# Modulation of all layers as VectorE sums, in halves, run through the mLSTM heads

## The chip, the cores and the metric

One core of a Trainium2 chip runs the whole network in one launch. The metric is the device time of that launch in microseconds. Three runs of the kernel before gave 2507.35, 2513.32 and 2513.51 us; the median is 2513.32. A further execution was profiled, and all rows below are from it.

## The reference, cut to what matters

Two blocks with two layers each process 512 tokens (256 context, 256 latent) of 1024 features, in float32. Block one has an mLSTM layer and a latent attention layer (MLA), each followed by a convolutional FFN; block two has two layers of token mixers, each followed by an MLP. Every layer is modulated by a condition vector: six vectors of 1024 features come from a matrix of 1024 x 6144.

```python
def _modulation(cond, w, b):
    m = jax.nn.silu(cond) @ w + b
    return jnp.split(m[:, None, :], 6, axis=-1)

def _modulate(x, shift, scale):
    return x * (1 + scale) + shift

# per layer: 0 shift, 1 scale, 2 gate of the mixer; 3 shift, 4 scale, 5 gate of the FFN
x = _layer_norm(ALPHA * x + ml[2] * yl, ...)
f = _conv_ffn(_modulate(x, ml[3], ml[4]), ...)
x = _layer_norm(ALPHA * x + ml[5] * f, ...)
```

Latent and context tokens have different conditions, so each vector is computed for two conditions where the context is still needed, else for one. The four matrices hold 96 MB, more than a quarter of what the kernel loads.

## The kernel before, in words

Activations lie transposed, features on the 128 partitions and tokens along the free dimension. Every float32 product is three matmuls of split operands (high and low part): `mm3`, lines 284 to 286. A weight comes in tiles of 512 KB: `weight` (line 266) loads the tile into one of five `raw` buffers by a DMA on SyncE's queue, ScalarE rounds it to the high part (line 278), VectorE subtracts to get the low part (line 279). Three buffers of split weights are shared by all, except for weights that are kept through two halves of the tokens (`keep`), which take room in the pool `ap` of 31 buffers of 4 KB per partition.

The layers are called 0 to 3 here. Their modulation is background work, written as Python generators. `weight` calls `tick(size)` between its load and its split: each call adds credit for the size of the weight (1 for 512 KB) times a rate, and for each whole credit the first generator in the list `bg` is run to its next `yield`. So one step of the modulation is put into the program order between a weight's load and its split. `finish(gen)` runs a generator to its end. A scheduler then orders the instructions of each engine by that program order and by its own estimate of when each is ready; every engine runs its instructions in order.

There are two forms of the background work. A part is one of the six vectors of a layer; its matrix slice comes in 8 chunks of 512 KB, each of 128 input features by 1024 output features.

- `ada_v` (line 430; layers 0, 1 and 3): for each condition an accumulator of 128 x 1024. Per chunk and condition one instruction, accumulator + chunk x condition value of the partition: on ScalarE for the first chunk (line 449), VectorE `scalar_tensor_tensor` for the other seven (line 451). With the last chunk, in the same step, comes the part's end: matmuls with ones of 128 x 32 (line 460), one per condition and 512 features, each on a column tile of its own, sum over the partitions into one PSUM bank (pool `pa`, one buffer); ScalarE copies it (line 464), four transposes (line 467) turn it, and VectorE adds the bias (line 472).
- `ada` (line 396; layer 2): per chunk four column-tiled matmuls of 128 x 32 by 128 x 256 straight from the chunk (line 410), accumulated in PSUM over the eight chunks; at the end a copy (line 416) and two transposes (line 419).

Layer 0's parts 0 and 1 are needed first and are made apart, in `first_mod`. Its parts 2 to 5 run beside the projections `w_up` (rate 0.6) and `w_og` (1.1). In front of the heads `pause` (line 492) runs the open part to its end and stops the background work, which goes on after the heads. Layer 1 runs in the first FFN (rate 0.8), layer 2 behind it in the MLA and the second FFN (1.2), layer 3 in the first MLP (0.8).

The mLSTM (`_mlstm`) projects, computes the gates by scans over time, and then per head: `qk_of` (8 weight tiles), `weights_of` (decay weights, VectorE and ScalarE), later `values_of` (8 tiles) and `head_out`. The gate row of a head is spread over the partitions by a matmul with a row-select table `selr` (line 718), an `ap` buffer copied from a 512 KB input (lines 688 to 691). `weights_of` leaves two `ap` buffers per head, one of them half full.

Of the kernel before, what the change touches and what calls it, by code (L numbers as in the profile page):

```python
# [8 lines left out]
F32 = mybir.dt.float32  # L9
F32R = mybir.dt.float32r  # L10
I32 = mybir.dt.int32
AF = mybir.ActivationFunctionType
ALU = mybir.AluOpType
AX = mybir.AxisListType

P = 128
D = 1024
T = 512
TC = 256
KD = D // P  # L20
# [10 lines left out]
_PV = {}  # L31
# [31 lines left out]
def _lay(I):  # L63
    I = {k: np.asarray(v) for k, v in I.items()}
    o = {}
# [67 lines left out]
    o["sel"] = _sel()  # L133
# [3 lines left out]
def _consts():  # L137

    s = np.arange(P)[:, None]
    j = np.arange(P)[None, :]  # L140
    m0 = np.where(s <= j, 0.0, -1e30)
    m1 = np.where(s >= j, 0.0, -1e30)
    perms = []
    for w in (16, 8):
        pm = np.zeros((P, P))
        for m in range(P):
            if m % (2 * w) < w:
                pm[m + w, m] = -1.0
            else:
                pm[m - w, m] = 1.0  # L150
        perms.append(pm)
    return np.concatenate([np.eye(P), m0, m1] + perms, 1).astype(np.float32)
# [17 lines left out]
def _sel():  # L170
    k = np.arange(P)[:, None, None]
    r = np.arange(8)[None, :, None]
    row = (r % 4) + 32 * (r // 4)
    return np.broadcast_to((k % 64) == row, (P, 8, P)).astype(np.float32)
# [5 lines left out]
class _K:  # L180
    def __init__(self, ctx, tc, A, out):
        self.tc, self.nc, self.A, self.out = tc, tc.nc, A, out
        nc = tc.nc
# [14 lines left out]
        self.credit = 0.0  # L198
        self.hold = self.open = False
# [3 lines left out]
        cst = cp.tile([P, 5 * P], F32, name="cst", tag="cst")  # L203
# [12 lines left out]
        self.mask = (cst[:, P:2 * P], cst[:, 2 * P:3 * P])  # L216

# [178 lines left out]
    def ada(self, l, parts=range(6), mod=None):  # L396


        nc = self.nc
        if mod is None:  # L400
            mod = self.cp.tile([P, 6, KD, 2], F32, name=f"mod{l}", tag=f"mod{l}")
        yield mod
        bo = _PV["ada_b"][0] + 48 * l
        for part in parts:
            ps = self.pa.tile([P, 512], F32, name=self.uid("pa"), tag="pa")
            for kt in range(KD):
                raw = self.rawp.tile([P, 4, 256], F32, name=self.uid("raw"), tag="raw")
                nc.sync.dma_start(raw, self.A["ada"][6 * l + part - 2, kt])
                for j in range(4):
                    nc.tensor.matmul(ps[32 * j:32 * j + 32, 0:256], self.cs[:, l // 2, kt, :],  # L410
                                     raw[:, j, :], start=(kt == 0), stop=(kt == KD - 1),
                                     tile_position=(0, 32 * j))
                if kt < KD - 1:
                    yield
            rows = self.t2()
            nc.scalar.copy(rows[:, 0:256], ps[:, 0:256])
            pt = self.ax_ps()
            for h in range(2):
                nc.tensor.transpose(pt[:, h * P:(h + 1) * P], rows[:, h * P:(h + 1) * P], self.ident)
            m = mod[:, part].rearrange("p (j h) w -> p h j w", h=2)  # L420
            b = self.pv[:, bo + part * KD:bo + (part + 1) * KD].rearrange("p (j h) -> p h j", h=2)
            t = pt[:, 0:256].rearrange("p (h j w) -> p h j w", h=2, j=4)
            for h in range(2):
                nc.vector.tensor_tensor(m[:, h], t[:, h, :, 0:2],
                                        b[:, h].unsqueeze(2).to_broadcast([P, 4, 2]), op=ALU.add)
            if part in (1, 4):
                nc.vector.tensor_scalar(mod[:, part], mod[:, part], 1.0, None, op0=ALU.add)
            yield

    def ada_v(self, l, parts=range(6)):  # L430
# [7 lines left out]
        for part in parts:  # L438
            conds = (1,) if l % 2 and part > 1 else (0, 1)
            nw = len(conds)  # L440

            acc = [self.a4(F32, (P, D)) for _ in conds]
            for kt in range(KD):
                raw = self.rawp.tile([P, D], F32, name=self.uid("raw"), tag="raw")
                nc.sync.dma_start(raw, self.A["ada"][6 * l + part - 2, kt].rearrange("p a b -> p (a b)"))
                for s, w in zip(acc, conds):
                    c = self.cs[:, l // 2, kt, w:w + 1]
                    if kt == 0:
                        nc.scalar.activation(s, raw, AF.Copy, scale=c)
                    else:  # L450
                        nc.vector.scalar_tensor_tensor(s, raw, c, s, op0=ALU.mult, op1=ALU.add)  # L451
                self.open = True
                if kt < KD - 1:
                    yield
            self.open = False

            ng = 32 * 2 * nw
            ps = self.pa.tile([P, 512], F32, name=self.uid("pa"), tag="pa")
            for i in range(2 * nw):
                nc.tensor.matmul(ps[32 * i:32 * i + 32], self.ones[:, 0:32],  # L460
                                 acc[i // 2][:, 512 * (i % 2):512 * (i % 2) + 512],
                                 start=True, stop=True, tile_position=(0, 32 * i))
            rows = self.t2()
            nc.scalar.copy(rows[0:ng], ps[0:ng])
            pt = self.ax_ps()
# [9 lines left out]
            yield  # L475

    def later(self, gen, rate):

        self.bg.append([gen, rate])

    def tick(self, size):
        if not self.bg or self.hold:
            return
        self.credit += self.bg[0][1] * size
        while self.bg and self.credit >= 1.0:
            self.credit -= 1.0
            try:
                next(self.bg[0][0])
            except StopIteration:
                self.bg.pop(0)  # L490

    def pause(self):

        while self.open:
            next(self.bg[0][0])
        self.hold = True

    def finish(self, gen):

        while any(g is gen for g, _ in self.bg):  # L500
            for _ in self.bg.pop(0)[0]:
                pass
# [87 lines left out]
def _mlstm(K, mod, rest):  # L590
# [38 lines left out]
    K.later(rest, 0.6)  # L629
# [8 lines left out]
    K.bg[0][1] = 1.1  # L638
# [49 lines left out]
    selr = K.a4(F32R, (P, 8, P))  # L688
    sel = K.a4(F32, (P, 8, P))
    nc.sync.dma_start(sel, A["sel"])  # L690
    nc.vector.tensor_copy(selr, sel)
# [19 lines left out]

    def weights_of(hd, qp):
# [3 lines left out]
        for d in range(2):  # L716
            ps = K.mm_ps()
            nc.tensor.matmul(ps, selr[:, 4 * d + hd, :], R2, start=True, stop=True)
# [58 lines left out]
        pt = [K.a4(), K.a4(F32, (P, 2, TC))]  # L777
# [75 lines left out]
    K.pause()  # L853
# [41 lines left out]
    K.hold = False  # L895
# [870 lines left out]
def _build(tc, A, out):  # L1766
    with ExitStack() as ctx:
# [7 lines left out]
        gen = K.ada_v(0, (2, 4, 3, 5))  # L1775
        mod = next(gen)
        z, yl = _mlstm(K, mod, gen)
# [4 lines left out]
        gen1 = K.ada_v(1)  # L1782
        mod1 = next(gen1)
        K.later(gen1, 0.8)
        gen2 = K.ada(2, (1, 0, 2, 4, 3, 5))
        mod2 = next(gen2)
        K.later(gen2, 1.2)
# [26 lines left out]
        for l in range(2):  # L1814
# [3 lines left out]
            if l == 0:  # L1818
                gen3 = K.ada_v(3)
                mod3 = next(gen3)  # L1820
                K.later(gen3, 0.8)
# [29 lines left out]
```

## Time and profile before

| | us |
|---|---|
| median of three runs (2507.35 to 2513.51) | 2513.32 |
| profiled execution, its own time | 2507.25 |
| span of the profiled execution | 2505.5 |
| TensorE (PE) busy | 2407.6 |
| VectorE (DVE) busy | 1619.3 |
| ScalarE (ACT) busy | 1109.9 |

The span runs from the first to the last instruction on the core. Busy times are sums over an engine's instructions, overlaps within the engine counted once. PE is the matmul part of TensorE, PEld its weight loads, SP the queue that issues the DMAs. An operation is written out<-in by the program's buffer names, L with a number is the line of the kernel. Matmuls are pipelined: their duration is longer than the distance between two starts.

### The profile page before, as it was taken

How to read it: one execution, taken by the hardware profiler on the slowest of the kernel's cores; microseconds unless marked ns; L12 is line 12 of the kernel's file. 1: busy time of each engine (PE TensorE's matmuls, PEld its weight loads, DVE VectorE, ACT ScalarE, POOL GpSimd, SP SyncE). 2: the span in 40 equal slices, each digit the busy share in tenths (PEclk: the TensorE clock that was granted, in tenths of full speed). 3: DMA queues.
4: the chain of work that ended last, by engine and by line, in shares of the span. 5: the costliest groups of instructions: out<-in, count | busy, mean ns of one | idle time of the engine just before them, and what ended most of it. 6: DMA issues, size and time to landing. Idle time of an engine off the chain costs nothing.

```text
span 2505.5 us, 36625 instructions
## 1 busy us (share of the span) xinstructions
PE 2407.6 (96%) x14362; PEld 2076.6 (83%) x14362; DVE 1619.3 (65%) x2953; ACT 1109.9 (44%) x1879; POOL 11.4 (0%) x20
## 2 busy tenths in 40 slices
PE   7998999999998999999999999989899999998998
PEld 5876888788897878878887999867888888977998
DVE  3867444544567756557676677797865556697665
ACT  4743333422445423235545456554523324465543
POOL 0000000000000000000000000000000000000000
PEclk9999999999999999999998999998899999998999
DMA  8676223433324554556337554222445455233553
GB/s 300 198 233 221 86 85 112 132 93 118 108 78 143 162 158 160 180 165 206 128 119 253 192 179 150 72 84 81 137 157 175 146 160 185 64 91 104 188 183 119
DMA packets 114750, 369.72 MB, mean 148 GB/s; under 512 B 12688, under 2 KB 17040, under 8 KB 114576
## 3 DMA queue, kind: packets, MB, share of 16 engines
q1 hardware_dynamic: 114576, 367.37, 45.0%
q8 instruction: 113, 1.85, 0.3%
q14 instruction: 61, 0.50, 0.1%
HBM read 357.88 MB, written 9.44 MB: 147 GB/s over the span
## 4 chain that ended last, share of the span: by engine, by line
PE 86%; DVE 5%; DMA 3%; ACT 3%; issue 2%; SPq 0%; DVEq 0%; ACTq 0%
PE pm L284 23%; PE pm L285 23%; PE pm L286 22%; PE px L284 4%; PE px L285 4%; PE px L286 4%; DMA raw<-in_ada 2%; DVE a L451 1%; PE px L1601 1%; PE pa L410 1%; PE px L310 1%; DVE wl L279 1%; PE pm L1192 1%; PE px L334 1%; DVE a L279 1%
## 5 line engine op out<-in xcount | busy, mean ns | idle before, releaser
L284 PE MATMUL pm<-a,wh 128*128 128x512 f32 (+1 forms) x2432 | 839.7, 347 | 6.6 <-DVE a L264 3.3
L286 PE MATMUL pm<-a,wl 128*128 128x512 f32 (+1 forms) x2432 | 834.5, 344 | 2.6 <-DVE wl L279 2.6
L285 PE MATMUL pm<-a,wh 128*128 128x512 f32 (+1 forms) x2432 | 836.9, 345 | 0.0
L278 ACT CAST wh<-raw 128x1024 fp32r<-128x1024 f32 (+2 forms) x421 | 420.1, 1002 | 800.1 <-PE pm L285 443.3
L279 DVE TENSOR_TENSOR wl<-raw,wh 128x1024 fp32r<-128x1024 f32 (+2 forms) x421 | 488.2, 1162 | 312.8 <-ACT wh L278 310.5
L284 PEld LDWEIGHTS pm<-a,wh 128*128 128x128 f32 x2432 | 463.3, 191 | 79.7 <-ACT wh L278 11.5
L286 PEld LDWEIGHTS pm<-a,wl 128*128 128x128 f32 x2432 | 463.8, 191 | 56.6 <-DVE wl L279 3.7
L285 PEld LDWEIGHTS pm<-a,wh 128*128 128x128 f32 x2432 | 464.8, 191 | 53.0 <-issue 1.6
L451 DVE SCALAR_TENSOR_TENSOR a<-raw,cs,a 128x1024 f32<-128x1024 f32 x168 | 211.0, 1281 | 91.3 <-DMA raw<-in_ada 89.2
L284 PE MATMUL pm<-a,a 128*128 128x256 f32 (+2 forms) x844 | 245.2, 303 | 16.9 <-ACT a L278 7.6
L285 PE MATMUL pm<-a,a 128*128 128x256 f32 (+2 forms) x844 | 248.8, 297 | 1.5 <-DVE a L279 0.9
L286 PE MATMUL pm<-a,a 128*128 128x256 f32 (+2 forms) x844 | 246.4, 295 | 0.4 <-DVE a L279 0.4
L284 PEld LDWEIGHTS pm<-a,a 128*128 128x128 f32 x844 | 162.8, 197 | 29.1 <-ACT a L278 10.1
L285 PEld LDWEIGHTS pm<-a,a 128*128 128x128 f32 x844 | 166.4, 197 | 4.4 <-DVE a L264 1.2
L286 PEld LDWEIGHTS pm<-a,a 128*128 128x128 f32 x844 | 165.8, 197 | 2.7 <-DVE a L279 0.6
L530 DVE SCALAR_TENSOR_TENSOR a<-pm,mod,a 128x256 f32<-128x256 f32 x188 | 87.3, 480 | 69.5 <-PE pm L286 68.6
L284 PE MATMUL pm<-wh,a 128*128 128x512 f32 (+1 forms) x336 | 128.1, 384 | 3.3 <-ACT a L263 3.3
L285 PE MATMUL pm<-wl,a 128*128 128x512 f32 (+1 forms) x336 | 129.3, 385 | 0.0
L263 ACT CAST a<-t 128x256 fp32r<-128x256 f32 (+2 forms) x173 | 86.1, 505 | 95.4 <-DVE t L1741 49.2
L286 PE MATMUL pm<-wh,a 128*128 128x512 f32 (+1 forms) x336 | 126.0, 383 | 0.0
L284 PE MATMUL px<-a,wh 128*128 128x256 f32 (+1 forms) x364 | 120.3, 331 | 0.0
L285 PE MATMUL px<-a,wh 128*128 128x256 f32 (+1 forms) x364 | 119.7, 330 | 0.0
(309 smaller groups left out, 2940.8 us busy)
## 6 DMA issues: line engine op xcount, KB each, us to landing
raw<-in_ada SPq DMA_DIRECT2D x192, 512.0 KB, 4.3
raw<-in_w_m SPq DMA_DIRECT2D x128, 512.0 KB, 4.2
raw<-in_ffn_in SPq DMA_DIRECT2D x88, 512.0 KB, 4.1
raw<-in_w_qk SPq DMA_DIRECT2D x32, 512.0 KB, 3.6
raw<-in_w_v SPq DMA_DIRECT2D x32, 512.0 KB, 3.5
raw<-in_ffn_oa SPq DMA_DIRECT2D x32, 512.0 KB, 3.6
raw<-in_w_inb SPq DMA_DIRECT2D x28, 512.0 KB, 3.5
raw<-in_w_up SPq DMA_DIRECT2D x16, 512.0 KB, 4.7
```

The lines of the kernel that those rows point to most:

```text
L263: self.nc.scalar.copy(hi, src)
L278: nc.scalar.copy(hi, raw)
L279: nc.vector.tensor_sub(lo, raw, hi.bitcast(F32))
L284: mm(out, ah, bh, start=start, stop=False)
L285: mm(out, ah, bl, start=False, stop=False)
L286: mm(out, al, bh, start=False, stop=stop)
L310: self.nc.tensor.matmul(out_ps[:, i * nt + t:i * nt + t + 1], a[:, c0 + t * P:c0 + (t + 1) * P], self.ones[:, 0:1], start=(k == 0), stop=( ...
L334: self.nc.tensor.transpose(ps[:, t * P:(t + 1) * P], col[:, t:t + 1].to_broadcast([P, P]), self.ident)
L410: nc.tensor.matmul(ps[32 * j:32 * j + 32, 0:256], self.cs[:, l // 2, kt, :], raw[:, j, :], start=(kt == 0), stop=(kt == KD - 1), tile_posi ...
L451: nc.vector.scalar_tensor_tensor(s, raw, c, s, op0=ALU.mult, op1=ALU.add)
L530: self.nc.vector.scalar_tensor_tensor(z[:, a:b], ps[:, a:b], gate[:, kt, w:w + 1], z[:, a:b], op0=ALU.mult, op1=ALU.add)
L1192: nc.tensor.transpose(pt[:, s * P:(s + 1) * P], p[:, s * P:(s + 1) * P], K.ident)
```

## The change

All layers use one generator, `ada`. A part with one condition is made as in `ada_v`. A part with two conditions is made in two halves of 512 features: a chunk is then 256 input features by 512 output features (again 512 KB, in pieces of 2 KB), the accumulator of both conditions is one `ap` buffer of 128 x 2 x 512, a chunk needs four sums of 512 columns, and each half has its own pair of sum matmuls into the same PSUM bank. The end is cut into steps: sums with the last chunk, the copy one step later, the transposes and bias another. Each `yield` names its price in credits, 1 for a chunk of one condition, 2.3 for one of two, 0.5 for the steps of the end; `tick` runs steps while the credit is positive, and caps it at 2.

Layers 0 and 1 are put in the list at the start, and `pause` is gone: the work runs on through the heads. The rate is a property of the stage: 0.8 in `w_up`, 2.2 in `w_og`, 1.3 in the heads, 0.8 in `w_mo`, 1.5 from the first FFN on (layer 2 joins there), 1.2 in the first MLP (layer 3). The row-select table becomes 8 columns of `consts`, broadcast along the free dimension as the matmul's stationary operand, and two heads share the half-full buffer.

```diff
-    return np.concatenate([np.eye(P), m0, m1] + perms, 1).astype(np.float32)
+    return np.concatenate([np.eye(P), m0, m1] + perms + [_sel()], 1).astype(np.float32)
...
-    def ada(self, l, parts=range(6), mod=None):
...
-    def ada_v(self, l, parts=range(6)):
+    def ada(self, l, parts=range(6)):
...
         for part in parts:
+            src = self.A["ada"][6 * l + part - 2].rearrange("k p a b -> p k (a b)")
             conds = (1,) if l % 2 and part > 1 else (0, 1)
             nw = len(conds)
...
+            ng = 64 * nw
+            ps = None
+            nk, nf = (1, D) if nw == 1 else (2, 512)
+            for f0 in range(0, D, nf):
+                acc = self.a4(F32, (P, nw, nf))
+                for k0 in range(0, KD, nk):
+                    raw = self.rawp.tile([P, nk, nf], F32, name=self.uid("raw"), tag="raw")
+                    nc.sync.dma_start(raw, src[:, k0:k0 + nk, f0:f0 + nf])
+                    for i, w in enumerate(conds):
+                        for k in range(nk):
+                            c = self.cs[:, l // 2, k0 + k, w:w + 1]
+                            if k0 + k == 0:
+                                nc.scalar.activation(acc[:, i], raw[:, k], AF.Copy, scale=c)
+                            else:
+                                nc.vector.scalar_tensor_tensor(acc[:, i], raw[:, k], c, acc[:, i],
+                                                               op0=ALU.mult, op1=ALU.add)
+                    yield nw + 0.3 * (nw - 1)
+                if ps is None:
+                    ps = self.pa.tile([P, 512], F32, name=self.uid("pa"), tag="pa")
+                for i in range(nw):
+                    for f in range(0, nf, 512):
+                        g = 64 * i + (f0 + f) // 16
+                        nc.tensor.matmul(ps[g:g + 32], self.ones[:, 0:32], acc[:, i, f:f + 512],
+                                         start=True, stop=True, tile_position=(0, g))
+                if f0 + nf < D:
+                    yield 0.5
             rows = self.t2()
             nc.scalar.copy(rows[0:ng], ps[0:ng])
+            yield 0.5
             pt = self.ax_ps()
...
-            yield
+            yield 0.5
...
     def tick(self, size):
-        if not self.bg or self.hold:
+        if not self.bg:
             return
-        self.credit += self.bg[0][1] * size
-        while self.bg and self.credit >= 1.0:
-            self.credit -= 1.0
+        self.credit = min(self.credit + self.rate * size, 2.0)
+        while self.bg and self.credit > 0.0:
             try:
-                next(self.bg[0][0])
+                self.credit -= next(self.bg[0])
...
-    def pause(self):
...
-    K.later(rest, 0.6)
+    K.rate = 0.8
...
-    K.bg[0][1] = 1.1
+    K.rate = 2.2
...
-    selr = K.a4(F32R, (P, 8, P))
-    sel = K.a4(F32, (P, 8, P))
-    nc.sync.dma_start(sel, A["sel"])
-    nc.vector.tensor_copy(selr, sel)
+    selr = K.sp.tile([P, 8], F32R, name="selr", tag="selr", bufs=1)
+    nc.vector.tensor_copy(selr, K.sel)
...
-            nc.tensor.matmul(ps, selr[:, 4 * d + hd, :], R2, start=True, stop=True)
+            nc.tensor.matmul(ps, selr[:, 4 * d + hd:4 * d + hd + 1].to_broadcast([P, P]), R2, start=True, stop=True)
...
-        pt = [K.a4(), K.a4(F32, (P, 2, TC))]
+        if hd % 2 == 0:
+            late[0] = K.a4(F32, (P, 4, TC))
+        pt = [K.a4(), late[0][:, 2 * (hd % 2):2 * (hd % 2) + 2]]
...
-    K.pause()
+    K.rate = 1.3
...
-    K.hold = False
+    K.rate = 0.8
...
-        gen = K.ada_v(0, (2, 4, 3, 5))
-        mod = next(gen)
-        z, yl = _mlstm(K, mod, gen)
+        gens = [K.ada(0, (2, 4, 3, 5)), K.ada(1), K.ada(2, (1, 0, 2, 4, 3, 5)), K.ada(3)]
+        mod, mod1, mod2, mod3 = (next(g) for g in gens)
+        gen, gen1, gen2, gen3 = gens
+        K.later(gen)
+        K.later(gen1)
+        z, yl = _mlstm(K, mod)
...
-        gen1 = K.ada_v(1)
-        mod1 = next(gen1)
-        K.later(gen1, 0.8)
-        gen2 = K.ada(2, (1, 0, 2, 4, 3, 5))
-        mod2 = next(gen2)
-        K.later(gen2, 1.2)
+        K.later(gen2)
+        K.rate = 1.5
...
-                gen3 = K.ada_v(3)
-                mod3 = next(gen3)
-                K.later(gen3, 0.8)
+                K.later(gen3)
+                K.rate = 1.2
```

## Rows read from the trace of the kernel before

**Rows 1.** The page: busy time by engine, and the chain's shares.
```profile
PE 2407.6 (96%) x14362; PEld 2076.6 (83%) x14362; DVE 1619.3 (65%) x2953; ACT 1109.9 (44%) x1879; POOL 11.4 (0%) x20
...
PE 86%; DVE 5%; DMA 3%; ACT 3%; issue 2%; SPq 0%; DVEq 0%; ACTq 0%
```
**Rows 2.** Table of stages: busy us (instructions) by engine, PEclk, DMA share, GB/s.
```profile
130.00:260.00 130.00, 122.15 (x546) 95.12 (x545) 89.19 (x96) 51.21 (x64) 0.00 (x0) 0.99 0.68 222
260.00:650.00 390.00, 386.69 (x1813) 323.29 (x1812) 178.97 (x312) 131.74 (x224) 0.00 (x0) 0.99 0.33 103
650.00:700.00 50.00, 48.81 (x232) 40.45 (x231) 39.66 (x66) 30.50 (x48) 0.00 (x0) 1.00 0.40 126
...
750.00:800.00 50.00, 39.98 (x289) 36.73 (x288) 44.40 (x81) 29.11 (x51) 0.00 (x0) 0.93 0.53 179
800.00:1110.00 310.00, 308.82 (x1401) 251.36 (x1401) 182.19 (x227) 102.15 (x128) 0.00 (x0) 1.00 0.48 153
1110.00:1350.00 240.00, 230.30 (x1715) 192.48 (x1713) 168.88 (x413) 128.56 (x266) 1.85 (x2) 0.96 0.50 167
...
1650.00:1700.00 50.00, 42.80 (x182) 32.84 (x181) 48.00 (x112) 23.00 (x47) 0.00 (x0) 0.86 0.13 37
```
**Rows 3.** Layer 2's old matmuls (L410) and transposes (L419): stage table sums; group.
```profile
sum 760.00, PE 34.09 PEld 9.39; mean PE 6.82 PEld 1.88
...
sum 760.00, PE 2.29 PEld 1.47; mean PE 0.46 PEld 0.29
...
L410 PE MATMUL pa<-raw,cs 128*32 128x256 f32 x328 | 30.1, 413 | 2.6 <-DMA raw<-in_ada 2.1 <-ACT t L416 0.5
```
**Rows 4.** Timeline of TensorE around a part's end: start, us, engine, operation.
```profile
880.17 0.39 PE L285 MATMUL px<-a,wh 128*128 128x512 f32 x1
880.40 0.39 PE L286 MATMUL px<-a,wl 128*128 128x512 f32 x1
880.72 1.06 PE L460 MATMUL pa<-a,hm 128*32 128x512 f32 x8
881.72 0.50 PE L284 MATMUL pm<-a,wh 128*128 128x512 f32 x1
...
987.57 1.05 PE L460 MATMUL pa<-a,hm 128*32 128x512 f32 x4
988.56 0.50 PE L284 MATMUL pm<-a,wh 128*128 128x512 f32 x1
...
139.12 0.39 PE L284 MATMUL pm<-a,wh 128*128 128x512 f32 x1
139.35 0.60 PE L467 MATMUL px<-cst,t 128*128 128x128 f32 x4
139.71 0.48 PE L285 MATMUL pm<-a,wh 128*128 128x512 f32 x1
```
**Rows 5.** Groups on VectorE by form: count | busy us, mean ns | idle before.
```profile
L451 DVE SCALAR_TENSOR_TENSOR a<-raw,cs,a 128x1024 f32<-128x1024 f32 x168 | 211.0, 1281 | 91.3 <-DMA raw<-in_ada 89.2 <-ACT a L449 1.8
...
L1614 DVE SCALAR_TENSOR_TENSOR t<-t,sd,t 128x512 f32<-128x512 f32 x16 | 11.9, 744 | 0.5 <-ACT t L1613 0.5
```
**Rows 6.** Timeline before the heads, two rows that waited [idle before, releaser].
```profile
225.59 1.04 ACT L278 CAST wh<-raw 128x1024 fp32r<-128x1024 f32 x1 [10.26 <-DMA raw<-in_w_qk]
...
227.18 1.11 PE L467 MATMUL px<-cst,t 128*128 128x128 f32 x4 [5.81 <-ACT t L464]
```
**Rows 7.** Table of stages, modulation sums (L451) alone, first LayerNorm.
```profile
750.00:800.00 50.00, 17.41 (x14) 0.93 0.53 179
```
**Rows 8.** Timeline of the DMA queue at the first MLP's end.
```profile
2076.36 4.57 SPq L445 DMA_DIRECT2D raw<-in_ada  x3
2082.41 23.59 SPq L271 DMA_DIRECT2D raw<-in_w_m  x7
```
**Rows 9.** DMA issues: count, KB each, median us to landing.
```profile
raw<-in_ada SPq DMA_DIRECT2D x192, 512.0 KB, 4.3
...
t<-in_xT SPq DMA_DIRECT2D x8, 256.0 KB, 2.9
```

More of the change, by code (lines that the diff above doesn't have):

```diff
@@ L132, in _lay @@
     o["consts"] = _consts()
-    o["sel"] = _sel()
     return {k: np.ascontiguousarray(v, dtype=np.float32) for k, v in o.items()}
@@ L170, in _sel @@
 def _sel():
[L171 to L174, printed above, removed]
+    k = np.arange(P)[:, None]
+    r = np.arange(8)[None, :]
+    return (k % 64) == (r % 4) + 32 * (r // 4)
 class _K:
@@ L197, in __init__ @@
         self.bg = []
-        self.credit = 0.0
-        self.hold = self.open = False
+        self.credit = self.rate = 0.0
         cp = self.cp
@@ L202, in __init__ @@
         nc.sync.dma_start(self.pv, A["pv"])
-        cst = cp.tile([P, 5 * P], F32, name="cst", tag="cst")
+        cst = cp.tile([P, 5 * P + 8], F32, name="cst", tag="cst")
         nc.sync.dma_start(cst, A["consts"])
@@ L216, in __init__ @@
         self.mask = (cst[:, P:2 * P], cst[:, 2 * P:3 * P])
+        self.sel = cst[:, 5 * P:5 * P + 8]
         self.cs = cp.tile([P, 2, KD, 32], F32, name="cs", tag="cs")
@@ L393, in first_mod @@
                                     op0=ALU.add, op1=ALU.add)
-    def ada(self, l, parts=range(6), mod=None):
[L399 to L413, printed above, removed]
-                    yield
[L415 to L428, printed above, removed]
-    def ada_v(self, l, parts=range(6)):
+    def ada(self, l, parts=range(6)):
         nc = self.nc
@@ L438, in ada_v @@
         for part in parts:
+            src = self.A["ada"][6 * l + part - 2].rearrange("k p a b -> p k (a b)")
             conds = (1,) if l % 2 and part > 1 else (0, 1)
             nw = len(conds)
[L442 to L462, printed above, removed]
+            ng = 64 * nw
+            ps = None
+            nk, nf = (1, D) if nw == 1 else (2, 512)
@@ L474, in ada_v, with later @@
                 nc.vector.tensor_scalar(mod[:, part], mod[:, part], 1.0, None, op0=ALU.add)
-            yield
-    def later(self, gen, rate):
-        self.bg.append([gen, rate])
+            yield 0.5
+    def later(self, gen):
+        self.bg.append(gen)
     def tick(self, size):
-        if not self.bg or self.hold:
+        if not self.bg:
             return
-        self.credit += self.bg[0][1] * size
-        while self.bg and self.credit >= 1.0:
-            self.credit -= 1.0
+        self.credit = min(self.credit + self.rate * size, 2.0)
+        while self.bg and self.credit > 0.0:
             try:
-                next(self.bg[0][0])
+                self.credit -= next(self.bg[0])
             except StopIteration:
                 self.bg.pop(0)
-    def pause(self):
-        while self.open:
-            next(self.bg[0][0])
-        self.hold = True
     def finish(self, gen):
-        while any(g is gen for g, _ in self.bg):
-            for _ in self.bg.pop(0)[0]:
+        while any(g is gen for g in self.bg):
+            for _ in self.bg.pop(0):
                 pass
@@ L587, in __getitem__, with _mlstm @@
         return self.ap[p, (c.start or 0) - self.lo:(T if c.stop is None else c.stop) - self.lo]
-def _mlstm(K, mod, rest):
+def _mlstm(K, mod):
     nc, A = K.nc, K.A
@@ L710, in qk_of @@
         return qp
+    late = [None]
     def weights_of(hd, qp):
```

## The prediction

> **What bounds the kernel now.** I read the page's engine line and its chain of waits first, then a table of stages, then single instructions. TensorE is busy 96% of the 2505.5 us span and carries 86% of the chain that ended last [rows 1]. So a microsecond of TensorE work taken out is worth about a microsecond; DMA or VectorE work counts only where TensorE waits for it. The stages [rows 2] show where that is. The mLSTM heads (260 to 650 us) lose almost nothing: TensorE 386.69 of 390. The three stages that lose are the gate stage before the heads (130 to 260, 122.15 of 130), the first LayerNorm (750 to 800, 39.98 of 50) and the attention block with the norms around it (1110 to 1350, 230.30 of 240, VectorE 168.88). The last line of the table, 1650 to 1700 us, shows what a VectorE-bound stage looks like here: VectorE 48.00 of 50, TensorE 42.80.
>
> **Part 1: layer 2 leaves TensorE.** The old matmul form of layer 2's modulation is busy 34.09 us on TensorE, its transposes 2.29 [rows 3]: 36.4 us go. They lie among matmuls of a full queue, so they are on the path. What comes back is the end of each part. An end's sums are column-tiled matmuls: from the last ordinary matmul before to the first behind takes 1.32 us (880.40 to 881.72), 0.23 of which is the ordinary matmul itself (880.17 to 880.40), so a group costs 1.09 us. A group of two matmuls costs the same: 0.99 us from its start to the next matmul (987.57 to 988.56), that of four 1.00 (880.72 to 881.72) [rows 4]. The four transposes take 139.12 to 139.71, less 0.23: 0.36 us. A part with both conditions now has two groups, one per half of the features: 2 x 1.09 + 0.36 = 2.54 us, six parts 15.2. Net: -21.2 us.
>
> **Part 2: the other layers pay for the halves.** Layer 0 has 4 parts with both conditions, layers 1 and 3 have 2 each; each gets a second group: 8 x 1.09 = +8.7 us. One-condition parts keep their single group.
>
> **Part 3: the end of layer 0 moves into the heads.** A chunk of a two-condition part costs 2.3 credits and such a part 8 x 2.3 + 1.5 = 19.9; a one-condition part 9. Before the heads 9 loads at 0.8 and 18 at 2.2 give 46.8 credits, so 19 of layer 0's 32 chunks are issued there; before, all 32 were, the last of them in one burst in front of the first w_qk weights. That burst has a price: ScalarE's weight cast waited 10.26 us for w_qk, the part's PSUM copy stood behind it on ScalarE, and TensorE, in order, sat 5.81 us at the transposes behind that copy [rows 6]. With no burst, and with the copy one load behind the sums and the transposes one behind the copy, I take this away: -5.8 us. What is late next there is the gate scan, which w_qk matmuls cover. If another load is late in its place, nothing is gained: bounds -5.8 to 0.
>
> In the heads 64 loads at 1.3 give 83.2 credits: 13 chunks of layer 0, 16 of layer 1's first two parts, 8 to 10 one-condition chunks. For a two-condition chunk there are four 512-wide sums. The nearest row of that form is the 512-wide scalar_tensor_tensor, 744 ns; the 1024-wide one takes 1281 [rows 5]. That is some 102 x 0.744 + 8 x 1.281 = 86 us more on VectorE, 178.97 + 86 = 265 of 390 (68%). In front of a weight's split stand then up to four sums (3.0 us). Three buffers of split weights hold two weights of TensorE work (each 24 matmuls of 0.23 us, 5.4 us), so that is covered; I take 0. Without any cover each of the 29 chunks would cost up to those 3.0 us; but beside the first FFN, with steps of one or two 1.281 us sums, TensorE lost 1.2 of 310 us [rows 2], so I bound it at +6. The part ends are counted above.
>
> Two halves cost 2 x 744 = 1488 ns where the whole costs 1281 [rows 5], so 14 two-condition parts x 28 sums x 0.744 + 56 x 1.281 = 363 us stand in place of 211.0: VectorE gets 152 us more. [...]
>
> **Part 4: where VectorE gets tight.** I follow the credits. (a) First half of w_mo (650 to 700): 6 one-condition chunks, 7.7 us; VectorE 39.66 + 7.7 = 47.4 of 50 [rows 2]. By the 1650 to 1700 line TensorE could fall from 48.81 to 42.80: bounds 0 to +6; the splits here are not a chain, I take +2. (b) First LayerNorm: 17.41 us of sums lie there now (14 instructions) [rows 7]; the six kept weights at 1.5 give 9 credits, 8 or 9 chunks of 1.281 us, plus those ahead of it: about the same. I take 0, bounds -5 to +5. (c) Attention block: 14 chunks of layer 2 instead of nearly all 48, but now on VectorE: 1.75 parts x 28 x 0.744 = 36 us. VectorE 168.88 + 36 = 205 of some 212 us (240 less 30.1 of matmuls and 2.6 of their waits, plus 4.6 of ends) [rows 2, 3]: 97%. At the share of the 1650 line (86%) TensorE's 203 us of work would take 237: +25. In its favour: these sums belong to no chain of the attention, half of them come with the loads ahead of it, and beside the first FFN such sums cost nothing now (800 to 1110: TensorE 308.82 of 310) [rows 2]. I take +5, bounds 0 to +25. The waits of the old matmuls for their chunks go: -2.6 [rows 3]. (d) End of layer 3: 57 loads at 1.2 give 68.4 of 75.8 credits, so 7 chunks are issued in one go in front of the last w_m2 weights; now 3 are, in 4.57 us, followed by 7 weights in 23.59 [rows 8]. Four more delay those weights by 4 x 1.5 = 6 us, at most 4 x 3.4 = 13.5. The first weights wait in five raw buffers anyway until the hidden layer frees room; I take +2, nearer to full cover, bounds 0 to +13.
>
> **At nothing:** 2 KB pieces instead of 4 KB in a two-condition chunk: the nearest rows are 4.3 us for a 512 KB chunk and 2.9 for a 256 KB load of 2 KB rows [rows 9]; two of those would be 5.8, +1.5 us of latency, covered by five raw buffers, and felt only where DMA is late. The row-select table's load and cast fall away behind w_qk matmuls. The PSUM bank held through two halves has no other user in these stages.
>
> **Sum:** -21.2 + 8.7 - 5.8 - 2.6 + 2 + 5 + 2 = -11.9 us. The profiled execution took 2507.25 us (span 2505.5 and 1.75 around it): 2495. It lies 6 us below the median of the runs shown (2513.32; fastest 2507.35), so the same sum on the median would be 2501; I keep to the profiled one, and the range has both.
>
> **Rivals.** (1) VectorE eats the attention's gain: (c) costs 13 to 22 instead of 5, all else as above: 2503 to 2512. For it: 97% load by the working. Against: sums beside the FFN cost TensorE nothing now. (2) Slower: VectorE's queue, in order, becomes the bound at both tight places, (a) +6 and (c) +25, and layer 3's burst delays the weights by its upper 13: -20.9 + 44 = +23, 2530 (-20.9 is the sum without collisions); with (c) at its bound alone and the rest as forecast, +8. The mechanism is one, sums ahead of splits and softmax steps on VectorE; it decides where VectorE passes some 95% of a stage. For it: the 1650 line. Against: most stages stay near 70%. (3) More is gained: no collision, and the first LayerNorm loses its waits for sums (-5): -20.9 - 5 and a few of the 7.9 us lost before the heads (130 less 122.15): 2472 to 2482. (4) It does not do what it says: TensorE was only filling waits of the attention with layer 2's matmuls. Then the 36.4 us give nothing: -11.9 + 36.4 = +24.5, 2532. Against: TensorE is 230.30 of 240 there.
>
> **Chances:** forecast 0.56 (2482 to 2503), rival 1 0.18, rivals 2 and 4 together 0.13, rival 3 0.13. The range 2475 to 2516 leaves out the outer part of rivals 2 to 4. About 0.3%, 7.5 us, is what a measurement can tell from no change. Faster: forecast, rival 3 and none of rival 1, 0.69; same: rival 1 and a little, 0.19; slower 0.12.
>
> **What would show it.** Right: no column-tiled matmuls over raw chunks in the profile after; 36 groups of sum matmuls of about 1.09 us (14 x 2 + 8); sums of 512 columns near 744 ns; the 5.81 us wait before the heads gone; heads still at 99%. Wrong: TensorE in the attention block below 93% with VectorE above 95%; a wait for w_m2 over 5 us at the end of the first MLP; TensorE idle at sum matmuls that wait for VectorE.

## The result, and the profile after

The change made the kernel slower, by 0.8%: 2531.9 us (median of four runs, 2526.24 to 2534.84) against 2511.06 (four runs, 2507.35 to 2513.51); the ratio is 1.0084, 95% interval 1.0061 to 1.0107. Forecast were 2495 us and a range of 2475 to 2516. The profiled execution took 2526.24 us, the fastest of the four, so its rows show rather less of the loss than the median.

The engine line answers to [rows 1]:

```profile
PE 2407.5 (95%) x14038; PEld 2078.1 (82%) x14038; DVE 1737.6 (69%) x3233; ACT 1129.1 (45%) x1917; POOL 11.4 (0%) x20
```

TensorE is busy for as long as before (2407.6 us), though the matmuls on raw chunks are gone. The groups of instructions, answering to [rows 3] and [rows 5], show where some of that time went:

```profile
L426 DVE SCALAR_TENSOR_TENSOR a<-raw,cs,a 128x512 f32<-128x512 f32 (+1 forms) x448 | 346.5, 811 | 116.7 <-DMA raw<-in_ada 101.7
L434 PE MATMUL pa<-a,hm 128*32 128x512 f32 x144 | 40.7, 615 | 2.7 <-DVE rs L321 2.7
L443 PE MATMUL px<-cst,t 128*128 128x128 f32 (+1 forms) x88 | 12.8, 270 | 0.3 <-ACT t L439 0.3
```

The sum matmuls of L434 are 36 groups at 40.7 / 36 = 1.13 us, close to the 1.09 forecast. In all, the modulation's matmuls and transposes are down from 64.4 us (34.1, 2.3, 19.0 and 9.0 for L410, L419, L460 and L467 before) to 53.5; the other 10.8 us are in the kernel's own matmuls, which are the same as before. That fits the granted clock, which is lower: 0.971 of full speed on average over the execution, where it was 0.976. Loss and gain are visible by stage, in the stages of [rows 2] moved to where they now lie (columns: stretch, its length, busy time and count of each engine, granted clock, DMA share, GB/s):

```profile
core 0: us, PE busy (x) PEld busy (x) DVE busy (x) ACT busy (x) POOL busy (x), PEclk, DMA share, GB/s
130.00:254.00 124.00, 124.00 (x550) 98.36 (x549) 80.34 (x111) 46.85 (x61) 0.00 (x0) 1.00 0.59 195
254.00:644.00 390.00, 385.95 (x1818) 315.45 (x1817) 248.14 (x425) 140.98 (x239) 0.00 (x0) 1.00 0.47 152
650.00:700.00 50.00, 44.63 (x201) 36.33 (x201) 33.74 (x56) 23.94 (x41) 0.00 (x0) 0.93 0.39 128
750.00:800.00 50.00, 45.14 (x337) 41.51 (x335) 45.80 (x101) 33.97 (x64) 0.00 (x0) 0.90 0.51 180
800.00:1118.00 318.00, 316.58 (x1453) 257.70 (x1452) 207.10 (x300) 109.41 (x148) 0.00 (x0) 1.00 0.41 136
1118.00:1366.00 248.00, 218.61 (x1431) 194.69 (x1430) 202.19 (x469) 136.65 (x276) 1.91 (x2) 0.93 0.35 113
```

The gate stage is now full, the heads still are. Two stages fell: 650 to 700, and above all the attention, from 230.30 of 240 us to 218.61 of 248, with the granted clock down from 0.96 to 0.93. VectorE is not at its limit there (202 of 248, 82%).

In the attention TensorE's longest wait is for the end of a LayerNorm's reciprocal root, a chain of short VectorE steps (TensorE rows, then VectorE rows; columns: start, duration, engine, line, operation, count, idle time before and what ended it):

```profile
1165.03 0.58 PE L309 MATMUL px<-hm,sq 128*128 128x1 f32 x4
1170.94 0.66 PE L333 MATMUL px<-cst,rs 128*128 128x128 f32 x2 [5.33 <-DVE rs L325]
```

```profile
1168.53 0.41 DVE L935 TENSOR_TENSOR a<-a,px 128x256 f32<-128x256 f32 x1
1168.86 0.16 DVE L319 TENSOR_SCALAR rs<-v 128x2 int32<-128x2 int32 x1
1168.93 0.41 DVE L263 TENSOR_TENSOR a<-hf,a 128x256 fp32r<-128x256 f32 x1
1169.27 0.41 DVE L936 TENSOR_TENSOR a<-a,px 128x256 f32<-128x256 f32 x1
1169.60 0.15 DVE L320 TENSOR_TENSOR rs<-rs 128x2 f32<-128x2 f32 x1
```

VectorE has no gap here: the steps of 0.15 us stand between the other half's LayerNorm work, and TensorE waits 5.33 us for their end. In the same stage before, all waits for this chain together were 1.0 us:

```profile
PE px L334 <- DVE rs L326: 1.0, 1, 1.0
```

The wait cost more than its own length, since the clock fell during it: from 1168.5 us it is granted at 0.50 of full speed for 10.2 us, and up to 1178.5 us the matmuls of 128 x 256 behind the wait start 0.21 us apart, then 0.12 (columns as in the table of stages):

```profile
1168.50:1178.70 10.20, 7.29 (x32) 6.78 (x33) 9.68 (x25) 8.53 (x14) 0.00 (x0) 0.50 0.60 180
```

No modulation sum stands near this wait, though: none runs on VectorE from 1146.2 to 1173.2 us. What differs is the order of the instructions. The second half's statistics (L534) start 11.05 us after the first half's, as they do in the kernel below that sums over a table; in all other kernels of this document they start 18.4 to 19.8 us after. With sums to place in the attention the scheduler chose another order; why, was not tried.

Further on sums do stand in the way. TensorE waits for a rotation (steps L1127, L1128, L1129 on VectorE, then a cast and a copy on ScalarE). The rows are VectorE's, then ScalarE's, then TensorE's:

```profile
1240.46 0.43 DVE L1128 TENSOR_TENSOR t<-t,a 128x256 f32<-128x256 f32 x1
1240.81 0.75 DVE L426 SCALAR_TENSOR_TENSOR a<-raw,cs,a 128x512 f32<-128x512 f32 x1
1241.47 0.68 DVE L278 TENSOR_TENSOR wl<-raw,wh 128x512 fp32r<-128x512 f32 x1
1242.07 0.74 DVE L426 SCALAR_TENSOR_TENSOR a<-raw,cs,a 128x512 f32<-128x512 f32 x1
1242.73 0.41 DVE L1129 TENSOR_TENSOR t<-t,t 128x256 f32<-128x256 f32 x1
```

```profile
1243.18 0.41 ACT L262 CAST a<-t 128x256 fp32r<-128x256 f32 x1 [5.25 <-DVE t L1129]
```

```profile
1243.91 1.22 PE L1125 MATMUL px<-t,cst 128*128 128x256 f32 x2 [2.38 <-ACT t L1252]
```

Two sums put 1.3 us between L1128 and L1129, which start 2.27 us apart; in the kernel without layer 2's sums (below) they start 0.45 to 1.27 us apart, and this wait is not there.

At 650 to 700 a sum stands in VectorE's order, waiting for its chunk, in front of splits that are ready, and TensorE waits for one of these (VectorE, then TensorE). These are sums of layer 1, which the change let run on here:

```profile
651.34 1.28 DVE L426 SCALAR_TENSOR_TENSOR a<-raw,cs,a 128x1024 f32<-128x1024 f32 x1 [5.97 <-DMA raw<-in_ada]
...
658.46 1.28 DVE L426 SCALAR_TENSOR_TENSOR a<-raw,cs,a 128x1024 f32<-128x1024 f32 x1 [3.50 <-DMA raw<-in_ada]
659.66 1.28 DVE L263 TENSOR_TENSOR a<-pm,a 128x512 fp32r<-128x512 f32 x2
```

```profile
661.59 0.80 PE L284 MATMUL px<-a,a 128*128 128x512 f32 x1 [3.49 <-DVE a L263]
```

VectorE kept to its order here: it is idle for 3.50 us, until 658.46, with a split behind the sum that has been ready since ScalarE's casts of these values (L262, 652.52 to 655.14 us).

### The profile page after: what moved, and what is told of

It reads as the page before. It is cut to its first block, busy times and chain, and to the rows that moved or that the text cites. A ratio compares the mean times of both kernels' runs of the same rounds, so it can differ in the third digit from the quotient of the medians.

```text
span 2524.5 us, 36326 instructions
## 1 busy us (share of the span) xinstructions
PE 2407.5 (95%) x14038; PEld 2078.1 (82%) x14038; DVE 1737.6 (69%) x3233; ACT 1129.1 (45%) x1917; POOL 11.4 (0%) x20
## 5 line engine op out<-in xcount | busy, mean ns | idle before, releaser
L426 DVE SCALAR_TENSOR_TENSOR a<-raw,cs,a 128x512 f32<-128x512 f32 (+1 forms) x448 | 346.5, 811 | 116.7 <-DMA raw<-in_ada 101.7
L262 ACT CAST a<-t 128x256 fp32r<-128x256 f32 (+2 forms) x173 | 86.2, 505 | 102.3 <-DVE t L1713 53.5
L283 PE MATMUL px<-a,wh 128*128 128x256 f32 (+1 forms) x364 | 120.5, 332 | 0.7 <-ACT a L262 0.5
L285 PE MATMUL px<-a,wl 128*128 128x256 f32 (+1 forms) x364 | 119.8, 330 | 0.0
```

The lines of the kernel that those rows point to most:

```text
L262: self.nc.scalar.copy(hi, src)
L283: mm(out, ah, bh, start=start, stop=False)
L285: mm(out, al, bh, start=False, stop=stop)
L426: nc.vector.scalar_tensor_tensor(acc[:, i], raw[:, k], c, acc[:, i], op0=ALU.mult, op1=ALU.add)
```

## The experiments

To place a difference I compare the start of the same single instruction in two profiles. All rows of this table show the change of a stretch's length against the kernel before, in us, worked out from such starts. The stretches: to the gate scan; heads to the third head's norm; to the fourth head's norm ("head 3"); to the second statistics of the first LayerNorm; first FFN, to the statistics at its end; attention, to the statistics behind it; second FFN; the rest.

```
kernel       gate  heads  head3    LN   FFN1  attn   FFN2  rest |  sum
after        -7.6    8.8    9.5  -3.4    6.8    2.1  -6.7  10.4 | 19.9
b_no_l2      -0.8   -0.1    0.0   0.0   -3.8  -14.3  -6.6   1.5 | -24.1
a_no_l2      -7.6    9.7    8.8  -3.4  -11.6  -14.2  -6.7   4.2 | -20.8
a_l2_pe      -4.2   11.7    9.1  -3.4   16.3   -7.3  -8.4  15.7 | 29.5
a_early      -4.5    9.6    8.7  -5.5    4.7  -12.0  -8.6   4.2 | -3.4
a_l2_ends    -6.2    9.8    7.8  -3.5    2.9   -9.8  -6.3  12.2 |  6.9
a_l2_nodma   -6.6    9.3    9.5  -3.4    6.3    2.7  -8.5  18.5 | 27.8
e_h3         -5.4   16.5    0.0  -6.1    5.8  -13.9  -6.3   8.4 | -1.0
e_l3         -6.4   11.5    7.3  -5.6    3.3  -13.9  -6.6   1.4 | -9.0
e_whole      -0.5    6.6    0.7  -4.1   12.7  -14.2  -6.5   4.8 | -0.5
e_all         1.2   11.9    2.1  -6.8   11.7  -14.2  -6.5   7.0 |  6.4
k1           -6.9    9.6    9.9  -6.9    5.3  -14.0  -6.5   7.2 | -2.3
k2           -7.4    7.2    0.5  -7.5   16.3  -10.0  -1.6  10.8 |  8.3
```

Each line is one execution; the last start lies shortly before the end, and behind it the kernel before takes 1.0 us longer than the others, so the sums are 1.0 above the difference of the spans. The rest differs by up to 14 us (4.2 to 18.5) between kernels with the same program text there, so I read nothing into that column. Much of this goes with the granted clock (0.95 and 0.96 over that stretch in the two rows further below): TensorE is busy for 912.3 to 922.4 us with the same 5640 matmuls. The gate column, too, goes from -4.2 to -7.6 between kernels with the same text. Medians, from four and more runs each, are beside the verdicts. The kernel before ran beside all of them, with medians of 2511.3 to 2512.3.

**Layer 2 left out.** In both kernels, before and after, the generator is replaced by constants (the lines are the kernel before's).

```diff
-        gen2 = K.ada(2, (1, 0, 2, 4, 3, 5))
...
+        nc.gpsimd.memset(mod2, 0.5)
```

> The kernel before, with layer 2's modulation left out (its coefficients are constants, its 48 chunks are not loaded). Theory A (the matmuls of layer 2 were on the path, and the change loses them again to VectorE sums that stand in front of LayerNorm and softmax steps): 36.4 us of TensorE work and 2.6 us of waits go, 2511 - 39 = 2472 us. Theory B (TensorE was filling waits of the attention with these matmuls): the waits stay, about 10 us go, 2500 us.

> The changed kernel, with layer 2's modulation left out in the same way. Attention and norms took 7.5 us more than before. Theory A: there the sums eat the 33 us that the matmuls gave, so 40 us come back, and 10 us for the sum matmuls beside the first FFN: 2532 - 50 = 2482 us. Theory B: the matmuls gave about 8 us there, so the sums cost 15, and 10 for the sum matmuls: 2507 us.

Measured: 2485.99 and 2487.26 us, ratios 0.9899 (0.9886 to 0.9912) and 0.9906 (0.9893 to 0.9918). The rest of the change is therefore worth nothing that can be measured, +1.3 us; all of the loss is layer 2's. As matmuls it cost 2511.3 - 2486.0 = 25.3 us, as sums 2531.9 - 2487.3 = 44.6. The second is less sure, some 6 us either way, since the interval of 2531.9 goes from 2526 to 2538. The 44.6 lie between the theories (50 and 25), nearer to A. The 25.3 lie between them too (39 and 10): part of the matmuls stood in waits. The stage table of the kernel before without layer 2 shows them uncovered:

```profile
1108.00:1332.00 224.00, 205.55 (x1412) 190.33 (x1412) 168.25 (x409) 131.07 (x266) 1.84 (x2) 0.95 0.28 90
```

TensorE now lacks 18.45 us of 224, where it lacked 9.7 of 240 with the matmuls [rows 2]. Between the starts that bound the attention in the table its idle time goes from 4.9 to 10.9 us, and its time at the lower clock from 7.6 to 13.4 us. So the old matmuls filled waits, and in that stage the clock was lower without them.

**Layer 2 on TensorE, at the new places.** The changed kernel with the old generator, each step priced like the new one's.

```diff
-        gens = [..., K.ada(2, (1, 0, 2, 4, 3, 5)), K.ada(3)]
+        gens = [..., K.ada_t(2, (1, 0, 2, 4, 3, 5), 2.3, 1.5), K.ada(3)]   # before's ada(), "yield 2.3"
```

> The changed kernel, only layer 2 on TensorE as in the kernel before, at the same loads (35 of its chunks beside the first FFN, 13 in the attention). Both theories: 35 x 0.71 + 1.6 = 26 us of matmuls beside the FFN in place of 10 us of sum matmuls, +16. Theory A: in the attention 9.5 us of matmuls in place of 40 us lost to sums, 2532 + 16 - 30 = 2518 us. Theory B: 13 chunks that cost some 2 us in place of 15, 2535 us.

Measured: 2527.08 us, ratio 1.0065 (1.005 to 1.008), between the two. Against the kernel without layer 2 that is 39.8 us, the full price of the prediction (36.4 + 2.6 = 39.0). By the table the 35 chunks beside the FFN cost 27.9 us (the expectation had 26) and the 13 in the attention 6.9 (9.5), against the kernel without layer 2; its profiled execution is the slowest of six, 9 us above the median. So matmuls beside the FFN, where TensorE has no waits to fill, cost all of their time; in their old places, 41 of 48 chunks behind it, layer 2 had cost 25.3 in all.

**Layer 2 done before the attention.**

```diff
         K.later(gen2)
-        K.rate = 1.5
+        K.rate = 2.2
```

> The changed kernel with 2.2 in place of 1.5 credits per load beside the first FFN, so that layer 2 is done before the attention, which then has no modulation in it. Theory A: 40 us come back in the attention, 4 us of sum matmuls go to the FFN: 2496 us. Theory B: the attention's waits are empty, 15 us come back: 2521 us. If 42 us more of sums beside the FFN (VectorE 207 + 42 of 318 us) make TensorE wait there, both are missed upward, and the profile's stage table shows it.

Measured: 2500.93 us, ratio 0.9959 (0.9948 to 0.9971): faster than before, by one number changed. 31 us come back, between the 11 and 36 that the theories give (2521 and 2496). Layer 2 now costs 2500.9 - 2487.3 = 13.7 us, no more than its part ends (15.2 by the prediction). Beside its sums in the FFN TensorE is 100% busy (first row), and the attention lost its load (second row):

```profile
970.00:1070.00 100.00, 100.00 (x442) 79.46 (x442) 75.69 (x112) 31.63 (x39) 0.00 (x0) 1.00 0.56 177
1125.00:1349.00 224.00, 205.83 (x1393) 190.67 (x1392) 167.35 (x407) 128.59 (x263) 1.84 (x2) 0.93 0.26 86
```

Where the waits in the attention were (engine, line, what it waited for, us in total, times, longest), for the changed kernel and for this one:

```profile
PE px L333 <- DVE rs L325: 7.2, 2, 5.3
PE pm L283 <- DVE a L263: 4.2, 3, 2.5
PE pm L283 <- ACT a L262: 3.8, 4, 2.0
PE px L1125 <- ACT t L1252: 2.9, 2, 2.4
```

```profile
PE pm L283 <- ACT a L262: 4.1, 2, 2.1
PE px L309 <- DVE ac L525: 3.0, 2, 2.4
...
PE px L333 <- DVE rs L325: 1.8, 1, 1.8
```

The wait for the reciprocal root falls from 7.2 to 1.8 us, the one for VectorE's splits of activations (L263) is gone.

**Sums, chunks and part ends apart.** One kernel loads the chunks and makes the ends without the sums, the other makes the sums over a table in SBUF without loading.

```diff
# a_l2_ends: first products (ScalarE), loads and ends stay
-                            else:
+                            elif l != 2:
                                 nc.vector.scalar_tensor_tensor(acc[:, i], raw[:, k], c, acc[:, i],
# a_l2_nodma
+                    if l == 2:
+                        raw = self.table.unsqueeze(1).to_broadcast([P, nk, nf])
+                    else:
```

> The changed kernel, where layer 2 loads its chunks and has its part ends (sum matmuls, copies, transposes), but the VectorE sums of layer 2 are left out (each accumulator keeps its first product). Theory (VectorE's own time in the chains of the attention costs): the 44.6 us that layer 2 costs in the changed kernel shrink to its part ends, at most 15.2 us: 2487 to 2502 us. Rival (chunk loads that hold back weight loads and the raw buffers, or the ends): most of it stays, 2520 us or more.

> The changed kernel, where layer 2's sums run in the same places over a table that is always in SBUF, and its 24 MB of chunks aren't loaded. Theory: the sums' time costs, not their waits for chunks (0.4 us of such waits in the attention in the trace): 2525 to 2532 us. Rival: VectorE, in order, stands at sums whose chunk is late, and that is what the others wait for: 2500 us or below.

Measured: 2512.18 us (ratio 0.9999, 0.9991 to 1.0008) and 2534.05 (1.009, 1.0077 to 1.0103). Without the loads nothing is gained against 2531.9, so neither the chunks' DMAs nor waits for them cost anything measurable for layer 2. Without the sums 19.7 us are gained, less than expected: 24.9 us stay with the ends. Of these 14.5 stand in the first FFN and 4.4 in the attention (table, against the kernel without layer 2), near the 15.2 forecast; 8.0 stand in the rest, where its text is the same. The two stage rows of that rest, with the ends and without layer 2, show what they are:

```profile
1540.40:2507.89 967.49, 917.96 (x5640) 810.85 (x5639) 676.54 (x1358) 442.20 (x784) 5.28 (x8) 0.95 0.38 125
1520.76:2480.19 959.43, 912.52 (x5640) 805.45 (x5639) 676.15 (x1357) 440.64 (x782) 5.28 (x8) 0.96 0.39 126
```

The same 5640 matmuls keep TensorE busy 5.4 us longer, at a lower granted clock (0.95 against 0.96; at the lower level for 94 us in place of 76). Whether layer 2 brings that about from so far away isn't shown.

Where the sums cost their time, the table alone doesn't tell. Its mark between FFN and attention is the first half's statistics, and in the two kernels with sums in the attention 59 more of TensorE's matmuls lie in front of it (first FFN by the table's marks, with sums and without):

```profile
774.36:1154.60 380.24, 372.03 (x1849) 308.81 (x1848) 260.26 (x411) 137.72 (x198) 0.00 (x0) 0.98 0.44 146
775.02:1151.34 376.32, 366.75 (x1790) 301.64 (x1789) 176.38 (x274) 136.43 (x194) 0.00 (x0) 0.98 0.44 148
```

So the table counts some 7 us of the attention's time (59 matmuls 0.12 us apart) under the FFN: its columns give the sums 6.8 - 2.9 = 3.9 us there and 2.1 + 9.8 = 11.9 in the attention. I compare instead the starts of the same of TensorE's own matmuls, of which every kernel has 13270 outside the modulation. With the sums it starts 0.7 us earlier than without at 780 us of the kernel without sums, 2.0 earlier at 1120 us, near the FFN's end, and 14.8 later at 1400 us, behind the attention. So the 126 sums beside the first FFN, 93.7 us of VectorE, cost nothing (-1.3 us), and the 42 in the attention, 31.2 us of VectorE, cost 16.8. The kernel with sums over a table shows the same (0.8 later, 0.1 earlier, 16.1 later).

**Three repairs on the early layer 2.** Head 3 kept free of modulation, layer 3 without its burst, and parts unsplit.

```diff
# e_h3
-    K.rate = 1.3
+    K.rate = 1.6          # heads; 0.0 from values_of(3) to the first half of w_mo
# e_l3
-                K.rate = 1.2
+                K.rate = 1.4
# e_whole
-            nk, nf = (1, D) if nw == 1 else (2, 512)
+            nk, nf = 1, D         # one accumulator buffer per condition
```

> Layer 2 early (2.2 credits per load beside the first FFN, 2501 us by the run before), and now no modulation from the value projection of head 3 to the first half of w_mo: the heads issue at 1.6 instead of 1.3 until then. Theory head 3 (a sum that waits for its chunk stands in VectorE's queue in front of the splits of the head outputs, 9.5 us): 2501 - 9.5 = 2491 us. Rival: the first LayerNorm behind it made 8 us good, and without the loss it doesn't, so the time only moves: 2500 us. If sums at 1.6 credits make the heads wait, they end later than in the changed kernel.

> Layer 2 early, and layer 3 at 1.4 instead of 1.2 credits per load, so that it is through before the last part of the first MLP and leaves no burst of 7 chunks in front of its last weights. Theory: the burst is the 5.4 us lost at the end of that MLP, and they come back: 2496 us. Rival: they are lost to the sums themselves, wherever they stand: 2501 us.

> Layer 2 early, and the parts with both conditions summed over all 1024 features in one, as before the change: one group of sum matmuls in place of two. Theory (the prediction's steps): 14 groups of 1.09 us go, 15 us, 2486 us; VectorE has 152 us less to do. Rival: most of the second groups stand in time that TensorE loses anyway, so that they give under 5 us: 2497 us. Above 15 us gained: VectorE's 152 us cost something beside the FFN too.

> All three on the early layer 2. If the gains add up: 2501 - 9.5 - 5.4 - 15 = 2471 us. With both rivals on the waits and only the sum matmuls gained: 2486 us. The kernel without layer 2's modulation took 2487 us, with the three losses in it.

Measured: 2500.74, 2500.13, 2509.31 (2504.13 to 2518.92) and 2514.27 us; against the kernel before 0.9964 (0.9952 to 0.9976), 0.996 (0.9948 to 0.9972), 0.9996 (0.9985 to 1.0006) and 1.0014 (1.0005 to 1.0022). The rival holds for the first two. At head 3 the loss is gone (8.7 to 0.0), but the heads, given more work, take 6.9 us longer. Without a burst ScalarE's cast at the end of the MLP is as late as with it (3.07 us waited in both, 3.28 in the changed kernel). Unsplit parts are slower, against every theory put down. The 152 us in my expectation were wrong as well, since they hold all of layer 2's sums, which the kernel before made on TensorE; VectorE's total falls only from 1739.6 to 1714.3. Heads and head 3 do get 11 us shorter, but the gate stage and the first FFN 12 longer, and VectorE stands longer at sums whose chunk has not come, first unsplit, then in halves:

```profile
DVE a L426 <- DMA raw<-in_ada: 168.8, 85, 7.1
```

```profile
DVE a L426 <- DMA raw<-in_ada: 106.3, 48, 5.7
```

Why the chunks are late there (two accumulators take two buffers of the pool instead of one) was not tried and stays open. All three changes together don't add up: 13.3 us slower than the early kernel, with the gate stage 5.7 and the first FFN 7.0 us longer than there, and only head 3 (6.6) and the LayerNorm shorter.

**Two other placements.**

```diff
# k1: K.rate = 0.0 from the second half of w_mo, then in the first FFN, after its kept weights
+            K.rate = 2.6
# k2: 0.0 from values_of(3), 2.2 there, 0.0 in the attention, 0.6 in the second FFN
```

> Layer 2 before the attention, and no modulation from the second half of w_mo through the first LayerNorm and the six kept weights of the FFN; 2.6 credits per load in the rest of that FFN, where TensorE was 100% busy in the run with 2.2. Theory (a sum costs only where VectorE stands in a chain that TensorE waits for): the LayerNorm's waits shrink by some 5 us against the run with 2.2 everywhere, 2496 us. Rival: 2.6 makes VectorE the bound of the FFN (76 of 100 us at 2.2), 2505 us or more.

> The heads at 1.3 up to head 2, then no modulation until the kept weights of the FFN are through; 2.2 in the rest of the first FFN, none in the attention, and the last 10 chunks of layer 2 at 0.6 in the second FFN. Theory: the 9.5 us at head 3 and some 5 of the LayerNorm come back, the second FFN gives 2: 2501 - 12 = 2489 us. Rival: sums cost about as much wherever they stand outside the attention, as the run with head 3 kept free showed: 2500 us.

Measured: 2502.84 us (0.9967, 0.9955 to 0.9979) and 2513.65 (1.0008, 0.9997 to 1.0019). Neither beats the early kernel. In k2 head 3 and the LayerNorm get 10 us shorter than in the early kernel, and the first FFN 11.6 and the second 7.0 longer; that part ends cost TensorE their time wherever it is full would fit, but was not taken apart here. The early kernel and the ones with head 3 kept free and with layer 3 at 1.4 are the fastest, within 1 us of each other and 0.4% under the kernel before.

## Why the prediction was wrong

The forecast was -11.9 us; the measured terms, by the medians, are 44.6 - 25.3 + 1.3 = +20.6. They part at three places.

1. **Layer 2 off TensorE** was put at 39.0 us (36.4 and 2.6 of waits), on the ground that TensorE was 96% busy there. It is worth 25.3: 13.7 too much. The step that failed is "they lie among matmuls of a full queue, so they are on the path": busy time was read as time on the path. When the matmuls were gone, 6.0 us of waits opened in the attention, and the clock was at its lower level for 5.8 us longer there; what made up the rest of the 13.7 isn't placed. Rival 4 named this and put the loss at all 36.4.
2. **Layer 2 as sums** was put at 15.2 for the ends and 5 for collisions, 20.2. It costs 44.6: 24.4 too little. The collisions, step (c), are 19.7 by the medians, 14.7 more than taken, and by the same matmuls of two profiles 16.8 in the attention and none beside the FFN. Step (c) took "beside the FFN such sums cost nothing" over to the attention. The row was right for the FFN (93.7 us of sums for nothing) and wrong for the attention (31.2 us for 16.8), where much of VectorE's work is in chains that TensorE waits for. The forecast expected trouble at 95% of VectorE; it came at 82%. Rival 2 named sums ahead of splits and softmax steps, and the bounds of 0 to 25 held; rows show sums ahead of a rotation, but the longest wait came with another order of the instructions and no sum near it, and how the 16.8 divide between the two stays open. The prediction has no term for the clock, which fell at the longest of these waits (5.33 us, with 10.2 us at half speed). The ends are 24.9, 9.7 more than taken, of which 8.0 lie in the rest at a lower clock. They are no fixed price: in the early kernel all of layer 2 costs 13.7.
3. **The rest** was put at 8.7 - 5.8 + 2 + 2 = +6.9 and came to +1.3. Inside it the terms went astray in both directions: the gate stage gave 7.6 (forecast 5.8) and the 5.81 us wait of [rows 6] is gone, the heads took 8.8 longer (forecast 0, bound 6), since seven groups of sum matmuls, 7.4 us, lie there now and none before, head 3 lost 9.5 (forecast 2, bound 6), the LayerNorm gave 3.4 (forecast 0), and the FFN got back what layer 1 had cost there (11.6 us without layer 2). That head 3's loss could be had back was not borne out: what was taken from there cost as much in the heads.

13.7 + 24.4 - 5.6 = 32.5 us, the distance from -11.9 to +20.6. Each of the first two alone uses up the forecast gain; the forecast gave the rivals that hold them, 2 and 4, 0.13 together. That their numbers, 2530 and 2532, meet the measured 2531.9 is luck: each has one of the two losses at its bound and the other as forecast.

Right were the prices of single instructions: 1.13 us per group of sum matmuls, 744 ns per 512-wide sum, 2 KB pieces at no cost (a chunk lands after 3.9 us in 2 KB pieces, 4.4 in 4 KB), the heads still full (385.95 of 390), the burst before the heads as a loss of its own. The halves, put at +8.7, could not be confirmed: the unsplit form gained nothing.

Of the marks that the prediction named for being wrong, the first appeared in one half: TensorE fell to 88% in the attention, under 93; VectorE did not pass 95. The wait for w_m2 did not appear: TensorE's longest there is 3.28 us, under 5. TensorE did stand at a sum matmul that waited for VectorE, for 2.7 us in all (the row of L434).

## What to carry to other kernels

Background work has two prices, its engine's and its place's. Here layer 2's independent matmuls were cheapest with 41 of 48 chunks behind the FFN, where part of them filled waits (25.3 us), and cost their full time with 35 beside a full TensorE (39.8 us); VectorE work was the other way round, free beside the FFN's long rows of matmuls (93.7 us of sums, -1.3 us) and dear in the attention (31.2 us for 16.8), where TensorE waits for short VectorE steps, at a VectorE load of 82%. Read such a loss between the same matmuls of two profiles: a new instruction can change the scheduler's order, and a mark of one's own can move with it. When work changes its engine, choose its place anew (here one rate, 1.5 to 2.2, turned +0.8% into -0.4%), and price what is removed by leaving it out once, not by its busy time.

## What the runs showed of the hardware

A sum of 1.28 us stands between two steps of 0.15 us that depend on each other twice inside one reciprocal root of the early kernel, without a gap on VectorE:

```profile
781.26 0.16 DVE L321 SCALAR_TENSOR_TENSOR rs<-rs,v 128x2 f32<-128x2 f32 x1
781.33 1.28 DVE L426 SCALAR_TENSOR_TENSOR a<-raw,cs,a 128x1024 f32<-128x1024 f32 x1
782.52 0.15 DVE L322 SCALAR_TENSOR_TENSOR rs<-rs 128x2 f32<-128x2 f32 x1
782.60 0.15 DVE L323 SCALAR_TENSOR_TENSOR rs<-rs 128x2 f32<-128x2 f32 x1
782.67 1.28 DVE L426 SCALAR_TENSOR_TENSOR a<-raw,cs,a 128x1024 f32<-128x1024 f32 x1
783.86 0.15 DVE L324 SCALAR_TENSOR_TENSOR rs<-rs 128x2 f32<-128x2 f32 x1
```

Leaving out the 24 MB of layer 2's chunks changed the time by nothing that can be measured (2534.05 against 2531.9 us): with 146 GB/s moved on average over the span of the changed kernel, its loss did not come from these loads.

The granted clock of TensorE is at one of two levels in every record of the kernel before (32) and of the changed one (38), full speed or half. In the changed kernel it fell at TensorE's waits of 3.49 us (ending at 661.59), 2.71 (789.44), 5.33 (1170.94) and 2.46 (1219.55), and was at half for 6.8, 10.2, 10.2 and 3.4 us. The matmuls behind them paid for these waits again: behind the first, those of 128 x 512 start 0.43 us apart at half speed and 0.23 at full, behind the last, those of 128 x 256 0.21 and 0.12.
